# One transformer block on one core: the first V products' squares, 1/rms and second V weights moved, and four small changes of order

## The chip, the cores and the metric

The kernel runs on one core of a Trainium2 chip, as one program. The metric is the device time of one execution in microseconds, as the median of several executions. In the text, PE is TensorE (the matrix engine), ACT is ScalarE, DVE is VectorE, POOL is GpSimd, and SP is SyncE, which issues most of the DMA transfers. P is 128, the number of partitions; SEQ is 512 tokens, in NT = 4 blocks of 128; D is 1024, in KB = 8 blocks of 128.

## The reference, cut to what matters

```
def layer(x, mem):                                   # x (1, 512, 1024), mem (1, 256, 1024), float32
    h = rms_norm(x, g_mix_pre)                       # x * rsqrt(mean(x*x) + eps) * g
    q_f, k_f, v_f, f_logit, q_c, k_c, v_c = split(h @ w_in)   # 512,512,512,8,512,512,512 columns
    log_f = log_sigmoid(f_logit + b_fgate)
    o_f = forgetting_attention(q_f, k_f, v_f, log_f)          # 8 heads of 64, causal
    o_c = chunked_rel_attention(q_c, k_c, v_c, rel_bias)      # 8 heads of 64
    mix = concat(rms_norm(o_f, g_fox_out), rms_norm(o_c, g_chunk_out)) @ w_out
    x = x + rms_norm(mix, g_mix_post)
    h, m = rms_norm(x, g_mem_pre), rms_norm(mem, g_mem_kv)
    ca = cross_attention(h, m, w_mem_q, w_mem_kv, w_mem_o)    # 4 heads of 256, 256 memory tokens
    x = x + rms_norm(ca, g_mem_post)
    h = rms_norm(x, g_ffn_pre)
    g, u = split(h @ w_gate_up)                               # 2 x 2816 columns
    return x + rms_norm((silu(g) * u) @ w_down, g_ffn_post)
```

## The kernel before

**Precision and products.** Every float32 operand of a product is held as two rounded halves, hi and lo (hi is a rounded copy, lo is the difference). `mm3` (line 139) issues three matmuls into one accumulator: hi times hi (L140), and the two mixed ones (L141, L142). For each weight block that arrives by DMA as `raw`, ACT casts the hi half (L125) and DVE subtracts to get the lo half (L126).

**Order.** The program is written as tile code. Tiles come from pools: a tag of a pool has a fixed number of buffers, and a tile that takes a buffer waits until the tile that held it before has been read for the last time. In PSUM there are 8 banks of 512 columns: tag a has three, s and t two each, o one. A scheduler lays the instructions of each engine into one fixed order by its own estimates of when they can run; `later(n)` and the place in the code shift it. At run time each engine goes through its list in order and waits at an instruction until what it reads is there.

**The first stage** (lines 224 to 355) computes the V products of the first head group and the forget gate's logits, before q and k. It needs no 1/rms for that, because 1/rms is a factor of each token that is applied afterwards. It goes through the 8 blocks of 128 features of x: `x_block` makes hTh and hTl (x times the gain, hi on ACT, lo on DVE), `v_weights` splits the 520 weight columns of the block into two halves, 264 and 256 columns wide (`vhi`, `vlo`), and `v_products` issues 24 matmuls per block into six accumulators: four of 264 columns (banks s, s, a, o) and two banks a that hold two of 256 each. Beside it, `squares` squares x on ACT into xs (L287), and the eight squared blocks are summed into one: five sums on POOL (L289), two on DVE (L321, L322). `feature_rstd` then multiplies the sum with a column of ones on PE (L251), adds eps on DVE (L146), raises to the power -1/2 on POOL (L147), and spreads the four columns of 1/rms over all partitions by four matmuls on PE (L258), which ACT copies to rrow (L327). The V accumulators are read out by ACT (L334) and DVE (L335), scaled by 1/rms. Six matmuls on a block of zeros (`still`) come first of all on PE (L237).

The weights of V take both buffers of the tags hi and lo of the pool wp. These are the buffers in which the weights of q and k are split afterwards.

**The attention stage.** `forget_gate` (L432 to 475) computes the log-sigmoid with Abs, Exp and Ln on ACT. A head then adds scores and bias on DVE (L519, which also gives the row's maximum nm), takes Exp on ACT (L529), scales on DVE (L531) and transposes on PE (L534). Exp, Ln and Silu lie in different function tables of ACT, which an ACT_TABLE_LOAD brings in ahead of the first instruction that uses another table.

**The FFN.** Gate and up are computed in column blocks of 256, n = 2 to 21, two for each u = n // 2 from 1 to 10. Those in EIGHT = (2, 3, 11) use eight products (96 matmuls), the others a Strassen-like scheme of seven products (`seven`, 84 matmuls). A `product` is four `mm3`, k = 0 to 3, of 128 x 256 each: its weights lie in a ring (ring_hi, ring_lo), its tokens in b or t1 to t4. ACT and DVE fill the ring ahead of PE (L902, L903), DVE also forms the sums of weights and of products. u = 0 is done apart from weights loaded earlier (first_ffn). The down projection follows; in two places it already cuts one matmul into two along its columns (L1229).

Of the kernel before, what the change touches and what calls it, by code (L numbers as in the profile page):

```python
# [14 lines left out]
P = 128  # L15
# [21 lines left out]
def hybrid_block_kernel(  # L37
# [189 lines left out]
    with tc.tile_pool(name="mix", bufs=1, reuse_waits="tile") as bp:  # L227
# [8 lines left out]
        for j in range(6):  # L236
            pe.matmul(warmed[:, :P], still, still, start=True, stop=True)  # L237
# [9 lines left out]
        def feature_rstd(sq, blocks, n, name):  # L247
# [7 lines left out]
            r = rstd_of(ss[:, :n], n, name)  # L255
# [5 lines left out]
            return r, rb[:, : n * P]  # L261

        vhi = [wp.tile([P, KB, n], F32R, tag="hi", name=f"vhi{n}", bufs=2) for n in (264, 256)]
        vlo = [wp.tile([P, KB, n], F32R, tag="lo", name=f"vlo{n}", bufs=2) for n in (264, 256)]
        halves = (slice(256, 520), slice(0, 256))

        def v_weights(raw, k, n):
            for j, cs in enumerate(halves):
                h = vhi[j][:, k : k + n, :]
# [4 lines left out]
            for j, cs in enumerate(halves):  # L274
                dve.tensor_tensor(
                    out=vlo[j][:, k : k + n, :], in0=raw[:, :, cs], in1=f32(vhi[j][:, k : k + n, :]), op=ALU.subtract
                )
# [8 lines left out]
        def squares(k, n):  # L286
            act.activation(xs[:, k : k + n, :], xt[:, k : k + n, :], AF.Square, scale=1.0 / 32.0)  # L287
            for j in range(max(k, 1), min(k + n, KB - 2)):
                pool.tensor_tensor(out=xs[:, 0, :], in0=xs[:, 0, :], in1=xs[:, j, :], op=ALU.add)  # L289

        def v_products(k):
            for t in range(NT):
                ts = slice(t * P, (t + 1) * P)
                mm3(acc0[t][:, :264], hTh[:, k, ts], hTl[:, k, ts], vhi[0][:, k, :], vlo[0][:, k, :], k == 0, k == KB - 1)
            for t in range(NT):
# [3 lines left out]
                    vhi[1][:, k, :], vlo[1][:, k, :], k == 0 and t % 2 == 0, k == KB - 1 and t % 2 == 1,  # L299
# [10 lines left out]
        for k, n in ((0, 1), (1, 1), (2, 2), (4, 2), (6, 2)):  # L310
# [123 lines left out]
        def forget_gate():  # L434
# [12 lines left out]
            act.activation(u, u, AF.Ln)  # L447
            dve.tensor_tensor(out=e, in0=e, in1=u, op=ALU.add)
# [126 lines left out]
        def mem_norm():  # L575
            mrow = feature_rstd(msq, range(2), 2, "rm")[1]
# [67 lines left out]
    with tc.tile_pool(name="cross", bufs=1, reuse_waits="tile") as cp:  # L644
# [163 lines left out]

        xr = mix
# [579 lines left out]
```

## Time and profile before

| | us |
|---|---|
| runs: lowest, median, highest of 3 | 779.17, 785.84, 786.11 |
| the profiled execution | 786.02 |
| its span, first to last instruction | 784.1 |
| outside the span | 1.9 |

The stages of the profiled execution follow one another as follows: first V products 5.7 to 35 us, q and k and the two attentions to about 245, memory projections, output projection and cross-attention to about 435, gate and up of the FFN 435 to 663, down 663 to 777, and the end to 784. A timeline row gives the start of an instruction from the span's start, its duration, engine, line, operation, output and inputs, shape, and how many neighbours of the same kind were joined; in brackets how long the engine had been idle before it, and what ended that. PE's instructions overlap in their records: the time that one costs in a stream is the distance from its start to the next one's start, called its step below.

### The profile page before, as it was taken

The numbers are of one execution on the slowest core, as the hardware profiler recorded it, in microseconds if no ns is written. First come the engines' busy times: TensorE is split into PE (matmuls) and PEld (weight loads), VectorE is DVE, ScalarE is ACT, GpSimd is POOL, SyncE is SP. The second block draws the span as 40 slices with busy tenths as digits, with TensorE's granted clock in tenths as the row PEclk, the third lists the DMA queues.
The fourth block names the chain that finished last, engine by engine and source line by source line (L and its number), as shares of the span: only waits on it lengthen the run. The fifth ranks groups of instructions, "written<-read, shape, count | busy, mean of one in ns | idle before, by whom it ended". The sixth has DMA issues, their size and how long they took to land.

```text
span 784.1 us, 12865 instructions
## 1 busy us (share of the span) xinstructions
PE 763.6 (97%) x4996; PEld 683.5 (87%) x4996; DVE 597.9 (76%) x1089; ACT 429.7 (55%) x781; POOL 70.9 (9%) x110
## 2 busy tenths in 40 slices
PE   8899999999999999999999999999999999999996
PEld 8887788888778988877778899999999999898985
DVE  5567889879887588645563778998899998987736
ACT  7358888757886348444553635554344446454421
POOL 6001231110321101000001100000000000000001
PEclk9999999999999999999999999999999999999999
DMA  6241212412312734421350202332433332323222
GB/s 245 79 137 54 55 55 67 130 67 82 114 60 96 276 107 163 131 72 64 107 171 18 81 28 81 108 109 81 135 109 108 108 109 77 111 92 124 89 74 107
DMA packets 60748, 80.05 MB, mean 102 GB/s; under 512 B 2704, under 2 KB 43664, under 8 KB 60688
## 3 DMA queue, kind: packets, MB, share of 16 engines
q1 hardware_dynamic: 59264, 74.49, 29.5%
q0 software_dynamic: 1280, 4.72, 1.6%
q8 instruction: 39, 0.64, 0.3%
q14 instruction: 21, 0.17, 0.1%
q10 hardware_dynamic: 144, 0.02, 0.0%
HBM read 77.13 MB, written 2.10 MB: 101 GB/s over the span
## 4 chain that ended last, share of the span: by engine, by line
PE 81%; ACT 6%; DVE 5%; issue 3%; DMA 2%; POOL 2%; SPq 0%; DVEq 0%; POOLq 0%; ACTq 0%
PE ps_a L141 15%; PE ps_a L142 15%; PE ps_a L140 15%; PE ps_s L140 5%; PE ps_s L141 5%; PE ps_s L142 5%; PE ps_t L141 2%; PE ps_t L140 2%; PE ps_t L142 2%; PE ps_o L140 2%; PE ps_o L141 2%; PE ps_o L142 2%; PE ps_t L534 2%; DMA raw<-in_dram 2%; PE ps_o L543 2%
## 5 line engine op out<-in xcount | busy, mean ns | idle before, releaser
L902 ACT CAST ring_hi<-fraw 128x1024 fp32r<-128x1024 f32 (+1 forms) x62 | 57.5, 931 | 65.1 <-DVE fraw L981 16.2
L126 DVE TENSOR_TENSOR lo<-raw,hi 128x1024 fp32r<-128x1024 f32 x56 | 68.2, 1223 | 22.2 <-ACT hi L125 21.8
L903 DVE TENSOR_TENSOR ring_lo<-fraw,ring_hi 128x1024 fp32r<-128x1024 f32 (+1 forms) x62 | 66.4, 1074 | 18.4 <-ACT ring_hi L902 17.9
L142 PE MATMUL ps_a<-hTh,lo 128*128 128x512 f32 x192 | 76.8, 400 | 0.6 <-DVE lo L126 0.6
L140 PE MATMUL ps_a<-hTh,hi 128*128 128x512 f32 x192 | 75.8, 395 | 0.2 <-ACT hi L125 0.2
L141 PE MATMUL ps_a<-hTl,hi 128*128 128x512 f32 x192 | 75.9, 395 | 0.0
L125 ACT CAST hi<-raw 128x1024 fp32r<-128x1024 f32 x56 | 57.8, 1048 | 23.8 <-PE ps_a L141 15.0
L902 ACT CAST ring_hi<-sums 128x1024 fp32r<-128x1024 f32 x34 | 35.7, 1049 | 52.5 <-PE ps_t L141 17.0
L903 DVE TENSOR_TENSOR ring_lo<-sums,ring_hi 128x1024 fp32r<-128x1024 f32 x34 | 41.4, 1218 | 4.0 <-ACT ring_hi L902 4.0
L142 PEld LDWEIGHTS ps_a<-hTh,lo 128*128 128x128 f32 x192 | 36.1, 188 | 7.3 <-DVE lo L126 1.0
L141 PEld LDWEIGHTS ps_a<-hTl,hi 128*128 128x128 f32 x192 | 36.1, 188 | 6.4
L140 PEld LDWEIGHTS ps_a<-hTh,hi 128*128 128x128 f32 x192 | 36.2, 188 | 6.0 <-ACT hi L125 0.4
L529 ACT ACTIVATE p<-p,nm 128x128 f32<-128x128 f32 (+1 forms) x64 | 36.1, 565 | 8.4 <-DVE nm L519 7.6
L140 PE MATMUL ps_a<-b,ring_hi 128*128 128x256 f32 x140 | 39.4, 281 | 0.0
L141 PE MATMUL ps_a<-b,ring_hi 128*128 128x256 f32 x140 | 39.3, 281 | 0.0
L142 PE MATMUL ps_a<-b,ring_lo 128*128 128x256 f32 x140 | 39.3, 281 | 0.0
L140 PE MATMUL ps_s<-b,ring_hi 128*128 128x256 f32 x128 | 36.0, 281 | 0.0
L141 PE MATMUL ps_s<-b,ring_hi 128*128 128x256 f32 x128 | 36.0, 281 | 0.0
L142 PE MATMUL ps_s<-b,ring_lo 128*128 128x256 f32 x128 | 36.0, 281 | 0.0
L536 ACT CAST pth<-ps_t 128x128 fp32r<-128x128 f32 (+1 forms) x64 | 27.1, 425 | 14.5 <-PE ps_t L534 13.7
L537 DVE TENSOR_TENSOR ptl<-ps_t,pth 128x128 fp32r<-128x128 f32 (+1 forms) x64 | 30.7, 486 | 5.1 <-ACT pth L536 3.8
L534 PE MATMUL ps_t<-ident,p 128*128 128x128 f32 x160 | 28.1, 275 | 1.1 <-DVE p L531 0.8
(541 smaller groups left out, 2642.5 us busy)
## 6 DMA issues: line engine op xcount, KB each, us to landing
raw<-in_dram SPq DMA_DIRECT2D x64, 512.0 KB, 3.7
fraw<-in_dram SPq DMA_DIRECT2D x62, 512.0 KB, 3.5
cb<-in_dram SPq DMA_DIRECT2D x8, 256.0 KB, 2.7
xo<-in_dram POOLq DMA_DIRECT2D x4, 512.0 KB, 5.4
out_dram<-yd SPq DMA_DIRECT2D x8, 256.0 KB, 2.0
rawv<-in_dram SPq DMA_DIRECT2D x3, 520.0 KB, 6.9
xt<-in_dram SPq DMA_DIRECT2D x3, 512.0 KB, 7.7
gb<-in_dram POOLq DMA_DIRECT2D x3, 512.0 KB, 4.4
```

What stands on the lines that cost most here:

```text
L125: act.copy(hi[:, j : j + n, :], raw)
L126: dve.tensor_tensor(out=lo[:, j : j + n, :], in0=raw, in1=f32(hi[:, j : j + n, :]), op=ALU.subtract)
L140: pe.matmul(dst, sh, mh, start=first, stop=False)
L141: pe.matmul(dst, sh, ml, start=False, stop=False)
L142: pe.matmul(dst, sl, mh, start=False, stop=last)
L529: act.activation(p[:, :n], p[:, :n], AF.Exp, bias=nm, scale=-1.0, accum_out=sm)
L534: pe.transpose(tp[:, k * P : (k + 1) * P], p[:, k * P : (k + 1) * P], ident)
L536: act.copy(span(ph, i), t3)
L537: dve.tensor_tensor(out=span(pl, i), in0=t3, in1=f32(span(ph, i)), op=ALU.subtract)
L543: pe.matmul(acc[:, a:], v[:, k, vh, :], m[:, k * PTS + a : k * PTS + SEQ], start=k == 0 and m is ph, stop=k == NT - 1 and m is pl,)
L902: act.copy(h2, v)
L903: dve.tensor_tensor(out=l2, in0=v, in1=f32(h2), op=ALU.subtract)
```

## The change

The change has one large part and four small ones.

1. **Squares, 1/rms and V weights.** The squares of x are taken in pairs of blocks (that of blocks 0 and 1 only when block 1 is there), and are added by three DVE additions of 128x1024 instead of five on POOL and two on DVE; two squared blocks are left, so that the product with ones is eight matmuls instead of four. These are issued after the V products of block 6, and the spread of 1/rms after those of block 7. The second half of the V weights (256 columns) goes into two tiles of four blocks each, in buffers of the tags T and Q of the attention's pool, so that one of the two buffers of hi and of lo is free for the first weights of q.
2. Ten matmuls on zeros at the start instead of six.
3. An Exp of one column directly behind the Ln of the forget gate.
4. A Silu of one column ahead of the stage of w_o.
5. In the FFN, for u = 1, 2, 4 and 7, the first L142 matmul of the gate's first product is cut into two matmuls of 128 columns.

```
-        for j in range(6):
+        for j in range(10):
...
-            r = rstd_of(ss[:, :n], n, name)
+            return rstd_of(ss[:, :n], n, name)
+
+        def spread(r, n):
...
-        vhi = [wp.tile([P, KB, n], F32R, tag="hi", name=f"vhi{n}", bufs=2) for n in (264, 256)]
-        vlo = [wp.tile([P, KB, n], F32R, tag="lo", name=f"vlo{n}", bufs=2) for n in (264, 256)]
+            return rb[:, : n * P]
+
+
+        vhi, vlo = (
+            [[wp.tile([P, KB, 264], F32R, tag=tag, name=f"v{tag}264", bufs=2)]]
+            + [[bp.tile([P, 4, 256], F32R, tag=own, name=f"v{tag}256_{j}", bufs=3) for j in range(2)]]
+            for tag, own in (("hi", "T"), ("lo", "Q"))
+        )
...
-        def squares(k, n):
-            act.activation(xs[:, k : k + n, :], xt[:, k : k + n, :], AF.Square, scale=1.0 / 32.0)
-            for j in range(max(k, 1), min(k + n, KB - 2)):
-                pool.tensor_tensor(out=xs[:, 0, :], in0=xs[:, 0, :], in1=xs[:, j, :], op=ALU.add)
+        def squares(k):
+            act.activation(xs[:, k : k + 2, :], xt[:, k : k + 2, :], AF.Square, scale=1.0 / 32.0)
+
+        def add_squares(k, other):
+            a = xs[:, k : k + 2, :]
+            dve.tensor_tensor(out=a, in0=a, in1=xs[:, other : other + 2, :], op=ALU.add)
...
-            if k < 4:
-                squares(k, n)
-            if k == 2:
-                squares(4, 2)
-                squares(6, 2)
-                dve.tensor_tensor(out=xs[:, KB - 2, :], in0=xs[:, KB - 2, :], in1=xs[:, KB - 1, :], op=ALU.add)
-                dve.tensor_tensor(out=xs[:, 0, :], in0=xs[:, 0, :], in1=xs[:, KB - 2, :], op=ALU.add)
+            if k:
+                squares(k if k > 1 else 0)
+            if k in (2, 6):
+                add_squares(k - 2, k)
+            if k == 6:
+                add_squares(0, 4)
             for j in range(k, k + n):
                 v_products(j)
-            if k == 4:
-                rcol, rps = feature_rstd(xs, (0,), NT, "rx")
-                act.copy(rrow, rps)
+                if j == 6:
+                    rcol = feature_rstd(xs, range(2), NT, "rx")
+        act.copy(rrow, spread(rcol, NT))
...
             act.activation(u, u, AF.Ln)
+            act.activation(warm, u[:, :1], AF.Exp)
...
+        act.activation(mix_ms[:, 0, 0:1], sm[:, :1], AF.Silu)
         xr = mix
...
+                pe.matmul(dst, w[0][:, k, :], b[:, 0, k, :], start=first and k == 0, stop=False)
+                pe.matmul(dst, w[0][:, k, :], b[:, 1, k, :], start=False, stop=False)
+                for to in parts:
+                    pe.matmul(dst[:, to], w[1][:, k, :], b[:, 0, k, to], start=False, stop=last and k == 3)
...
+            whole, parts = (slice(0, 256),), IN_STEP if u in (1, 2, 4, 7) else (slice(0, 256),)
```

DVE's list in the first stage, from the lo half of x of blocks 2 and 3 on. Before (L281 is that lo half, L275 the lo half of the V weights, L321 and L322 the additions of squares):

```order
L281 SCALAR_TENSOR_TENSOR hTl<-xt,gn,hTh 128x512 x2
L275 TENSOR_TENSOR vlo_110<-rawv_119,vhi_108 128x528
L275 TENSOR_TENSOR vlo_111<-rawv_119,vhi_109 128x512
L281 SCALAR_TENSOR_TENSOR hTl<-xt,gn,hTh 128x512
L321 TENSOR_TENSOR xs<-xs 128x512
L281 SCALAR_TENSOR_TENSOR hTl<-xt,gn,hTh 128x512
L322 TENSOR_TENSOR xs<-xs 128x512
L275 TENSOR_TENSOR vlo_110<-rawv_251,vhi_108 128x528
L275 TENSOR_TENSOR vlo_111<-rawv_251,vhi_109 128x512
```

The same stretch of DVE now (L291 and L285 are the lo halves, L301 the additions, L126 the lo half of the first q weights):

```order
L291 SCALAR_TENSOR_TENSOR hTl<-xt,gn,hTh 128x512 x2
L301 TENSOR_TENSOR xs<-xs 128x1024
L285 TENSOR_TENSOR vlo_115<-rawv_125,vhi_112 128x528
L285 TENSOR_TENSOR vlo_0_116<-rawv_125,vhi_0_113 128x512
...
L285 TENSOR_TENSOR vlo_115<-rawv_248,vhi_112 128x528
L285 TENSOR_TENSOR vlo_1_117<-rawv_248,vhi_1_114 128x512
L301 TENSOR_TENSOR xs<-xs 128x1024
L285 TENSOR_TENSOR vlo_115<-rawv_307,vhi_112 128x528
L285 TENSOR_TENSOR vlo_1_117<-rawv_307,vhi_1_114 128x512
L301 TENSOR_TENSOR xs<-xs 128x1024
L126 TENSOR_TENSOR lo_427<-raw_0_428,hi_426 128x1024
L126 TENSOR_TENSOR lo_427<-raw_4_432,hi_426 128x1024
```

No addition stands directly ahead of the third pair of weight halves (blocks 4 and 5) any more, one stands ahead of the second pair (blocks 2 and 3), and the lo halves of q's first weights have come forward to the end of the V weights.

PE's list around the product of the squares with ones, before (ps_s, ps_a and ps_o are V accumulators, L251 the product with ones, L258 the spread):

```order
L142 MATMUL ps_a_100<-vhi_109,hTl 128x256
L251 MATMUL ps_t_309<-ones,xs 128x1 x4
L140 MATMUL ps_s_95<-vhi_108,hTh 128x264
L141 MATMUL ps_s_95<-vlo_110,hTh 128x264
L142 MATMUL ps_s_95<-vhi_108,hTl 128x264
L140 MATMUL ps_s_96<-vhi_108,hTh 128x264
L258 MATMUL ps_t_317<-ident,rx_314 128x128 x4
L141 MATMUL ps_s_96<-vlo_110,hTh 128x264
```

The same rows of PE now, with the 24 V products of block 7 in between, and the first q product (hi_426, lo_427) behind them:

```order
L142 MATMUL ps_a_100<-vhi_1_114,hTl 128x256
L251 MATMUL ps_t_344<-ones,xs 128x1 x8
L140 MATMUL ps_s_95<-vhi_112,hTh 128x264
...
L142 MATMUL ps_a_100<-vhi_1_114,hTl 128x256
L260 MATMUL ps_t_380<-ident,rx_353 128x128 x4
L140 MATMUL ps_a_446<-hTh,hi_426 128x512
L141 MATMUL ps_a_446<-hTl,hi_426 128x512
L142 MATMUL ps_a_446<-hTh,lo_427 128x512
```

Four matmuls stood between the product with ones and the spread; now a whole block of 24 does, and the spread is the last thing ahead of q.

ACT's list where the first head begins, before (fb is the bias of a head, p its scores):

```order
L459 CAST c_605<-fc 8x512
L485 ACTIVATE fb_0_626<-ps_s_624,ct 128x128
L485 ACTIVATE fb_1_631<-ps_s_624,ct 128x256
L485 ACTIVATE fb_2_636<-ps_s_624,ct 128x384
L485 ACTIVATE fb_3_641<-ps_s_624,ct 128x512
L529 ACT_TABLE_LOAD
L529 ACTIVATE p_0_649,sm_651<-p_0_649,nm_650 128x128
```

And ACT's list at the forget gate now, some twenty rows earlier (fe and fu are its small tiles, L458 the Ln, L459 the new Exp):

```order
L451 ACTIVATE fe_588<-z 128x32
L452 ACTIVATE fe_588<-fe_588 128x32
L458 ACT_TABLE_LOAD
L458 ACTIVATE fu_589<-fu_589 128x32
L459 ACT_TABLE_LOAD
L459 ACTIVATE warm_93<-fu_589 128x1
L417 ACTIVATE Q_473<-qk 64x512 x2
```

The table load has left the head's first Exp and stands behind the Ln, ahead of the scaling of Q.

PE's list at the start of u = 2 in the FFN now (the gate's first product; before, the third row was one matmul of 128x256):

```order
L1084 MATMUL ps_a_5080<-b_4278,ring_hi 128x256
L1085 MATMUL ps_a_5080<-b_4278,ring_hi 128x256
L1087 MATMUL ps_a_5080<-b_4278,ring_lo 128x128 x2
L1084 MATMUL ps_a_5080<-b_4278,ring_hi 128x256
L1085 MATMUL ps_a_5080<-b_4278,ring_hi 128x256
```

Nothing else moves there: the neighbours and their sizes are those of before, and one matmul has become two.

## Rows read from the trace of the kernel before

**Rows 1.** The page, busy time of each engine (share of the span, instructions).

```profile
PE 763.6 (97%) x4996; PEld 683.5 (87%) x4996; DVE 597.9 (76%) x1089; ACT 429.7 (55%) x781; POOL 70.9 (9%) x110
```

**Rows 2.** Waits of PE, whole span: total, times, longest, in us.

```profile
PE ps_s L515 <- DVE nm L519: 1.7, 3, 1.2
```

**Rows 3.** First stage: length, busy of PE, PEld, DVE, ACT, POOL; granted clock, DMA.

```profile
1.05:3.98 2.93, 2.93 (x12) 2.63 (x12) 0.00 (x0) 1.65 (x3) 0.32 (x2) 1.00 0.63 212
3.98:5.67 1.69, 0.00 (x0) 0.03 (x1) 1.10 (x4) 1.08 (x2) 0.00 (x0) 1.00 1.00 316
5.67:9.29 3.62, 3.62 (x16) 3.62 (x17) 3.24 (x7) 3.02 (x6) 1.94 (x5) 1.00 0.98 358
9.29:18.92 9.63, 9.63 (x82) 9.63 (x81) 6.29 (x8) 8.63 (x14) 8.94 (x11) 1.00 0.69 243
```

**Rows 4.** Timeline of PE at the third pair of V weights.

```profile
18.93 0.28 PE L140 MATMUL ps_s<-vhi,hTh 128*128 128x264 f32 x1
20.27 0.39 PE L141 MATMUL ps_s<-vlo,hTh 128*128 128x264 f32 x1 [1.06 <-DVE vlo L275]
```

**Rows 5.** Timeline of DVE over the additions of squares and V weights.

```profile
10.97 2.06 DVE L275 TENSOR_TENSOR vlo<-rawv,vhi 128x528 fp32r<-128x528 f32 x2 [0.41 <-ACT vhi L273]
...
18.91 0.69 DVE L322 TENSOR_TENSOR xs<-xs 128x512 f32<-128x512 f32 x1 [2.90 <-POOL xs L289]
...
22.06 1.30 DVE L275 TENSOR_TENSOR vlo<-rawv,vhi 128x528 fp32r<-128x528 f32 x2
```

**Rows 6.** Timeline of PE from the product with ones to the spread.

```profile
26.06 0.95 PE L251 MATMUL ps_t<-ones,xs 128*128 128x1 f32 x8
...
27.32 0.28 PE L140 MATMUL ps_s<-vhi,hTh 128*128 128x264 f32 x1
28.39 1.16 PE L258 MATMUL ps_t<-ident,rx 128*128 128x128 f32 x8 [0.78 <-POOL rx L147]
```

**Rows 7.** Timeline of PE from the last V product into q.

```profile
34.56 0.28 PE L142 MATMUL ps_a<-vhi,hTl 128*128 128x256 f32 x1
...
36.32 0.50 PE L142 MATMUL ps_a<-hTh,lo 128*128 128x512 f32 x1 [0.59 <-DVE lo L126]
```

**Rows 8.** Timeline of all engines at the first Exp of the heads.

```profile
66.58 1.28 ACT L529 ACT_TABLE_LOAD   x1
...
67.88 0.40 ACT L529 ACTIVATE p<-p,nm 128x128 f32<-128x128 f32 x1
...
68.40 0.16 DVE L530 RECIPROCAL rc<-sm 128x1 f32<-128x1 f32 x1 [2.27 <-ACT p L529]
...
69.01 0.50 PE L515 MATMUL ps_s<-T,Q 128*128 128x512 f32 x1 [1.22 <-DVE nm L519]
```

**Rows 9.** Timeline of ACT at the first Silu.

```profile
457.12 1.28 ACT L1095 ACT_TABLE_LOAD   x1 [3.95 <-PE ps_a L142]
```

**Rows 10.** Busy time by stretches of gate and up, and of down (columns as in rows 3).

```profile
484.08:663.34 179.26, 179.26 (x1524) 179.26 (x1523) 164.40 (x238) 87.74 (x132) 0.00 (x0) 1.00 0.32 102
686.05:709.05 23.00, 23.00 (x205) 23.00 (x204) 18.87 (x31) 12.52 (x18) 0.00 (x0) 1.00 0.34 115
```

**Rows 11.** Timeline of PE at the first cut in down.

```profile
685.36 0.33 PE L1229 MATMUL ps_s<-ring_hi,latex 128*128 128x128 f32 x2
685.53 0.33 PE L140 MATMUL ps_s<-ring_hi,latex 128*128 128x256 f32 x1
685.71 0.28 PE L141 MATMUL ps_s<-ring_lo,latex 128*128 128x256 f32 x1
```

**Rows 12.** Timeline of PE at the last weights' arrival ahead of u = 1.

```profile
455.45 0.41 PE L141 MATMUL ps_a<-b,gate_w 128*128 128x256 f32 x2
455.70 0.28 PE L142 MATMUL ps_a<-b,gate_w 128*128 128x256 f32 x1
```

**Rows 13.** Busy time by stretches of 20 us, gate and up, then down.

```profile
600.00:620.00 20.00, 20.00 (x173) 20.00 (x171) 19.03 (x28) 9.42 (x14) 0.00 (x0) 1.00 0.34 107
680.00:700.00 20.00, 20.00 (x156) 19.11 (x155) 19.47 (x36) 11.28 (x16) 0.00 (x0) 1.00 0.21 72
```

More of the change, by code (lines that the diff above doesn't have):

```diff
@@ L268, in v_weights @@
             for j, cs in enumerate(halves):
-                h = vhi[j][:, k : k + n, :]
+                h = at_block(vhi[j], k, n)
                 if k == 0:
@@ L275, in v_weights @@
                 dve.tensor_tensor(
-                    out=vlo[j][:, k : k + n, :], in0=raw[:, :, cs], in1=f32(vhi[j][:, k : k + n, :]), op=ALU.subtract
+                    out=at_block(vlo[j], k, n), in0=raw[:, :, cs], in1=f32(at_block(vhi[j], k, n)), op=ALU.subtract
                 )
@@ L298, in v_products @@
                     acc1[t // 2][:, (t % 2) * 256 : (t % 2 + 1) * 256], hTh[:, k, ts], hTl[:, k, ts],
-                    vhi[1][:, k, :], vlo[1][:, k, :], k == 0 and t % 2 == 0, k == KB - 1 and t % 2 == 1,
+                    at_block(vhi[1], k)[:, 0, :], at_block(vlo[1], k)[:, 0, :], k == 0 and t % 2 == 0, k == KB - 1 and t % 2 == 1,
                 )
@@ L575, in mem_norm @@
         def mem_norm():
-            mrow = feature_rstd(msq, range(2), 2, "rm")[1]
+            mrow = spread(feature_rstd(msq, range(2), 2, "rm"), 2)
             for k in range(KB):
@@ L1065, in hybrid_block_kernel, with product @@
                         )
-        def product(dst, w, b, first=True, last=True):
+        def product(dst, w, b, first=True, last=True, parts=(slice(0, 256),)):
             for k in range(4):
-                mm3(dst, w[0][:, k, :], w[1][:, k, :], b[:, 0, k, :], b[:, 1, k, :], first and k == 0, last and k == 3)
+                if k:
+                    parts = (slice(0, 256),)
+                pe.matmul(dst, w[0][:, k, :], b[:, 0, k, :], start=first and k == 0, stop=False)
+                pe.matmul(dst, w[0][:, k, :], b[:, 1, k, :], start=False, stop=False)
+                for to in parts:
+                    pe.matmul(dst[:, to], w[1][:, k, :], b[:, 0, k, to], start=False, stop=last and k == 3)
+        IN_STEP = (slice(0, P), slice(P, 256))
         left, right = slice(0, 256), slice(256, 512)
@@ L1081, in up_eight, with eight @@
             return done
-        def eight(tags, done):
+        def eight(tags, done, parts):
             accs = [bank(tag) for tag in tags]
@@ L1089, in eight @@
                     for n, ns in enumerate((left, right)):
-                        product(accs[m][:, ns], w, bs[n], half == 0 and n == 0, half == 1 and n == 1)
+                        begin = half == 0 and n == 0
+                        product(accs[m][:, ns], w, bs[n], begin, half == 1 and n == 1, *([parts] if begin and m == 0 else []))
                     if half:
@@ L1118, in twice, with seven @@
             return bass.AP(a.tensor, a.offset, [list(a.ap[0]), [0, 2], list(a.ap[-1])])
-        def seven(O, tags, done):
+        def seven(O, tags, done, parts):
             p17, p26, p35, p4 = (bank(tag) for tag in tags)
@@ L1124, in seven @@
             (a11,) = take()
-            product(p17[:, left], a11, b11)
+            product(p17[:, left], a11, b11, parts=parts)
             act.copy(v, p17[:, left])
@@ L1160, in hybrid_block_kernel @@
         for u in range(1, FB // 2):
+            whole, parts = (slice(0, 256),), IN_STEP if u in (1, 2, 4, 7) else (slice(0, 256),)
             if 2 * u in EIGHT:
-                eight(("a", "a"), gate_eight)
+                eight(("a", "a"), gate_eight, parts)
             else:
-                seven(G, ("a", "a", "a", "o"), gate_seven)
+                seven(G, ("a", "a", "a", "o"), gate_seven, parts)
             dst = hidden(u)
             if 2 * u + 1 in EIGHT:
-                eight(("s", "s"), up_eight(dst))
+                eight(("s", "s"), up_eight(dst), whole)
             else:
-                seven(U, ("s", "s", "t", "t"), up_seven(dst))
+                seven(U, ("s", "s", "t", "t"), up_seven(dst), whole)
             keep(u, dst)
```

6 lines of the change are left out of this document (4 added, 2 removed).

## The prediction

> **What bounds the kernel now.** I read the page's busy times first: PE is busy for 97% of the span, DVE for 76%, ACT for 55% [rows 1]. So the end is set by PE, and only three things can move it: a wait of PE that goes, a matmul that becomes cheaper or superfluous, and a step (start to next start) that gets shorter at the same shape. The view of PE's waits comes next; its longest entry is 1.7 us in three times, one of 1.2 us [rows 2]. No wait is large, so the change is worth what its small waits add up to, and each has to be read from a timeline. Waits hide one thing: PE that works slowly counts as busy. So I also divided the length of long stretches by their matmuls, and found two speeds twice, at the start [rows 3] and in the FFN [rows 10].
>
> **V products: what goes.** Four losses stand in the first stage.
>
> Clock. The first 16 matmuls took 3.62 us, 0.226 each, the 82 records behind them 9.63, about 0.12 each with the records at the edges taken off [rows 3]. Columns of 256 and 264 in 0.22 us are the lower of PE's two clock levels (1.2 GHz), in 0.11 to 0.12 the upper (2.4 GHz), though the granted clock is printed as 1.00 in all four rows. Ahead of the 16, PE had worked for 2.93 us on zeros (twelve records) and then stood for 1.69. With four more matmuls on zeros, at 2.93/6 = 0.49 each, that gap shrinks by 1.95, so to nothing. I expect the upper level from about the first real matmul: 16 x (0.226 - 0.120) = 1.7, of which 0.3 is the start of the stream itself, leaves 1.4. Bounds: 0, if the clock rises no earlier, and 1.7.
>
> Third pair of weights. One step of 1.34 us instead of 0.12, and 0.1 for the slow restart [rows 4]: 1.3. The chain behind it is on DVE: the weights' lo half stood behind the addition L322, which had waited 2.90 us for POOL [rows 5]. That addition is now elsewhere and POOL is out of it.
>
> 1/rms. The spread waited for POOL's power: 28.39 - 27.32 = 1.07 instead of 0.12 [rows 6], 0.95. Now 24 matmuls, 2.9 us, stand between the product with ones and the spread, against the 2.3 us that the same way took here (26.06 to 28.39). I take 1.0 with the restart.
>
> Start of q. From the last V product to the third q matmul 1.76 us passed [rows 7], for one V step (0.12) and two of 512 columns (twice 0.23, double the 256-column steps of rows 10): 1.18 lost, because q's weights could only be split when V's buffers were free. They are now split before V ends. Something of a new product's start stays: 1.1.
>
> **V products: what comes.** The product with ones has twice the matmuls: 0.95 more [rows 6], take 0.9. The DVE additions cost PE nothing where a weight half isn't late for it: three of 128x1024, which I put at 1.2 each by the subtraction of 1,040 columns in 1.30 (22.06, rows 5). The tight place is block 2. By hand, with the clock up, PE ends block 1 near 11.6 and first takes six hi matmuls of block 2, to 12.35; its lo half is done near 12.3, since an addition stands ahead of it but the half itself takes 0.65 without POOL's additions, where it took 1.03 beside them (half of 2.06, against half of 1.30, rows 5). Cost 0, up to 1 if the addition is late. The squares are complete near 20.7 and PE asks at 26.2. The sum is 1.4 + 1.3 + 1.0 + 1.1 - 0.9 = **3.9 us** (2.0 to 4.8).
>
> **Exp table.** The load takes 1.28 us ahead of the first head's Exp; DVE and then PE wait for that chain, PE for 1.22 us [rows 8]. Moved behind the Ln, it stands ahead of the scaling of Q, which the heads read only after it, on an ACT that is busy for 55% of the span [rows 1]. Gain **1.25** (0, if another wait takes its place, to 1.4).
> The Trainium skill ("ScalarE: Activation LUTs", section "What ACT_TABLE_LOAD costs") states a drain of about 1.38 us beside the 1.28 of the load itself. Here the next ACTIVATE starts 1.30 us behind the load's start (67.88 after 66.58, rows 8), so no drain shows and I count the load alone; by the page the sum would be 1.4 us better.
>
> **Silu table.** At its old place ACT had been idle for 3.95 us and PE isn't made to wait [rows 9], so moving it saves nothing. At the new one it stands in the end of the cross-attention, where it delays a copy that w_o's products follow; other w_o products are put ahead of these. Cost between 0 and the load's own 1.28: take **-0.2**, since PE's list has cover there.
>
> **The cuts in the FFN.** The same 128x256 matmul has two steps. From 484.08 to 663.34 PE took 1,522 matmuls (1,524 records less two that overlap the edges) in 179.26 us: 117.8 ns. From 686.05 to 709.05 it took 203 in 23.00: 113.3 ns [rows 10]. Neither stretch has a wait. What happened just ahead of the second: a matmul was cut into two of 128 columns (685.36), and soon behind it the steps are 0.11 [rows 11]. What put PE into the longer step is two matmuls in 0.25 at 455.45, a short delay; from there on it is 0.12 [rows 12]. I read this as two rhythms of weight load and matmul, of which an odd step in the stream picks one, and which then holds until the next disturbance. The cut is placed at u = 1, 2, 4, 7. If it puts PE into the short rhythm for u = 2 to 10, the gain is 1,522 x 4.5 ns = 6.85. Each cut costs: 685.36 to 685.71 is 0.35 for two matmuls' work against 0.236, so 0.11, four times 0.45. u = 1 (241 matmuls, 1.1 us) I leave out: its cut may stand ahead of the disturbance at 455.45.
> DVE takes something back. It was busy for 19.03 of 20 us from 600 to 620 [rows 13]; PE 3.8% faster wants the same in 19.24. That just fits, but u = 2 and 3 and the passage into down (19.47 of 20, rows 13) don't leave room: 0.5, between 0 and 2. Sum 6.85 - 0.45 - 0.5 = **5.9** (3.5 to 7.5).
>
> **The total.** 3.9 + 1.25 - 0.2 + 5.9 = 10.85 from the profiled execution's 786.02: **775.2 us**. That execution lies 0.2 above the median of the runs (785.84), so nothing is corrected. One of the three runs gave 779.17, 6.7 below the median, which is just what the short rhythm would save in gate and up; I read it as the kernel falling into that rhythm by chance, and as a sign that it can be held.
>
> **Rivals.**
> *The cuts don't choose the rhythm.* For it: one cut followed by short steps is one case, and rhythms may be set by where operands lie or by a later DVE wait. Then the FFN gives -0.45 instead of 5.9 and the time is 775.2 + 6.35 = 781.5. Chance 0.17.
> The Trainium skill ("TensorE: Matmul & The Clock Gate", section "Back-to-back issue gap") gives a single gap of N/2.4 + 2.5 ns: 109 ns for 256 columns and 112 for two of 128, so a cut could only cost, which is this rival's result. The trace shows two steps for one shape (113.3 and 117.8, rows 10) where that rule has one, so I give it less weight than the row.
> *A cut turns the rhythm rather than setting it.* Then u = 2 and 3 run short, u = 4 to 6 long, u = 7 to 10 short: (336 + 672) x 4.5 ns = 4.5 less 0.45: 1.8 less gain, 777.0. Against it speaks that nothing in the trace shows a cut that ends the short rhythm. 0.08.
> *DVE becomes the bound.* With PE in the short rhythm from 484 on, weights for down come too late around 660 to 701, where DVE has only half a microsecond in 20 left [rows 13]. A wait also throws PE back into the long rhythm until the next cut. I price it at 2.5 us more than counted: 777.7. 0.10.
> *Slower: the squares hold PE.* The eight matmuls with ones now stand in PE's list ahead of all of block 7, and wait for the third DVE addition, which is behind the weights of blocks 6 and 7 and their Square on ACT. From 26.2 us on, each us by which that addition ends later is lost in full. It eats the change's whole gain when it ends at 37, and I see it end near 20.7, so this needs DVE or a DMA to be 16 us later than before: time 787 or more. 0.03.
> That the clock doesn't rise earlier gives 776.6 and lies within the forecast.
>
> **How the numbers follow.** The forecast itself has 0.62. What can be told from no change is 1%, 7.86 us: faster below 778.0, slower above 793.7. Faster collects the forecast (0.62), the turning rhythm (0.08) and about half of the DVE rival (0.05): 0.75. Same is 0.22, slower 0.03. The low end takes the good ends of all terms, 4.8 + 1.4 + 0 + 7.5 = 13.7, so 772.3, rounded to 772.0; the high end must hold the first rival: 781.6. What is left out is the slower rival, above, and the first rival together with a bad V stage.
>
> **What would show it.** In the changed kernel's profile: the first V matmuls step 0.12 and not 0.22; no wait of PE for the lo half near 18 us or for 1/rms; q's first matmul near 31.8 instead of 35; PE's wait for nm behind the first Exp gone; no new wait near 393; the stretch from u = 2 to u = 10 at 113 ns per matmul, some 172.5 us long; no waits of PE for ring_lo there or at 690. The prediction is wrong if that stretch still shows 118, or if its rows show PE idle behind DVE.

## The result, and the profile after

The changed kernel took 776.87 us (median of 8 runs, 776.01 to 778.97), the kernel before 786.07 beside it (8 runs, 779.17 to 789.06): a ratio of 0.9886, 95% interval 0.9870 to 0.9902, so faster by 1.1%. The forecast was 775.2, with a range of 772.0 to 781.6. The profiled execution took 778.66, at the slow end of its eight, with a span of 776.9 instead of 784.1.

The page's busy times of the changed kernel: PE works 3.7 us less, and its share has risen from the 97% of [rows 1] to 98%.

```profile
PE 759.9 (98%) x5016; PEld 680.2 (88%) x5016; DVE 598.1 (77%) x1090; ACT 429.2 (55%) x782; POOL 63.8 (8%) x105
```

**First stage.** PE's timeline of the changed kernel, with the first V product, the product with ones, the spread, and the first q product. These answer to [rows 4, 6, 7].

```profile
6.47 0.78 PE L140 MATMUL ps_s<-vhi,hTh 128*128 128x264 f32 x2 [0.78 <-DVE vhi L281]
...
28.64 1.84 PE L251 MATMUL ps_t<-ones,xs 128*128 128x1 f32 x16
...
33.30 1.05 PE L260 MATMUL ps_t<-ident,rx 128*128 128x128 f32 x8
34.16 0.47 PE L140 MATMUL ps_a<-hTh,hi 128*128 128x512 f32 x1
```

From 6.47 to 34.16 no row has a wait in brackets: the waits for the third pair of weights, for 1/rms and for q's weights are gone. But the first product starts 0.8 later than the 5.67 of [rows 3], and the clock has not come earlier. The stretch of [rows 3] in the changed kernel (length, busy of PE, PEld, DVE, ACT and POOL, then the granted clock, the DMA share and GB/s):

```profile
5.67:9.29 3.62, 2.84 (x14) 2.85 (x14) 3.62 (x9) 3.62 (x7) 0.69 (x3) 1.00 1.02 379
```

14 matmuls began in the 2.82 us after 6.47, about 0.2 each, which is the lower clock level (1.2 GHz), although the row prints a granted clock of 1.00, as [rows 3] did. Why the product starts late is seen on DVE (the first row is the kernel before, the second the changed kernel) and on POOL of the changed kernel:

```profile
5.24 0.49 DVE L271 CAST vhi<-rawv 128x264 fp32r<-128x264 f32 x2
```

```profile
4.99 1.52 DVE L281 CAST vhi<-rawv 128x264 fp32r<-128x264 f32 x2
```

```profile
4.72 0.52 POOL L395 MEMSET L<- 64x512 f32 x1
5.18 0.52 POOL L466 MEMSET fzero<- 8x512 f32 x1
5.65 0.52 POOL L470 MEMSET c<- 128x512 f32 x1
```

Two casts of 128x264 take 1.52 us while POOL fills tiles with zeros; in the kernel before POOL stood waiting for the squares then, until 7.29, and they took 0.49. This side of taking the additions off POOL I had not priced.

**Exp table.** ACT's timeline at the first head: the Exp follows the bias directly, with no load between them, as there was in [rows 8]. The bias began at 64.78 in the kernel before (first row below), so the first stage has given 1.7 us up to here.

```profile
64.78 1.78 ACT L485 ACTIVATE fb<-ps_s,ct 128x128 f32<-128x128 f32 x4 [1.96 <-PE ps_s L480]
```

```profile
63.09 1.78 ACT L497 ACTIVATE fb<-ps_s,ct 128x128 f32<-128x128 f32 x4 [2.00 <-PE ps_s L492]
64.75 0.42 ACT L541 ACTIVATE p<-p,nm 128x128 f32<-128x128 f32 x1
```

**Silu table.** ACT's timeline, then PE's, at the end of the cross-attention. The load pushes the last cast of the probabilities back, and PE's step from 392.99 to 393.47 is 0.48 instead of 0.23: 0.25 us lost.

```profile
390.50 1.28 ACT L821 ACT_TABLE_LOAD   x1
...
392.84 0.58 ACT L806 CAST pt<-ps_t 128x512 fp32r<-128x512 f32 x1
```

```profile
392.99 0.40 PE L140 MATMUL ps_a<-woh,oT 128*128 128x512 f32 x1
393.47 0.50 PE L140 MATMUL ps_o<-pt,vm 128*128 128x512 f32 x1
```

**Gate and up.** Busy times by stretches, u = 1 and then u = 2 to 10, as in [rows 10]:

```profile
452.94:481.68 28.74, 28.74 (x247) 28.74 (x245) 22.34 (x25) 11.00 (x14) 0.00 (x0) 1.00 0.22 65
481.68:654.80 173.12, 173.12 (x1527) 172.97 (x1526) 162.33 (x235) 86.65 (x131) 0.00 (x0) 1.00 0.34 106
```

u = 1 ran at 117 ns per matmul, the rest at 113.5 (173.12 over 1,525 records, three of them second halves of cut matmuls): 6.1 us less than the 179.26 of before. The cut at u = 4 in PE's timeline stands inside a stream that is already short and stays short:

```profile
519.78 0.28 PE L1085 MATMUL ps_a<-b,ring_hi 128*128 128x256 f32 x1
519.89 0.33 PE L1087 MATMUL ps_a<-b,ring_lo 128*128 128x128 f32 x2
520.06 0.33 PE L1084 MATMUL ps_a<-b,ring_hi 128*128 128x256 f32 x1
...
520.47 0.28 PE L1084 MATMUL ps_a<-b,ring_hi 128*128 128x256 f32 x1
```

From 519.89 to 520.47 four matmuls' work takes 0.58 instead of 0.45, so the cut costs 0.13; the next 512 steps are 0.113 again. So a cut doesn't turn the rhythm. The profiles of all kernels with cuts agree: behind u = 1's first product, a cut found PE in the long step (117.4 to 117.8) eight times and in the short one 24 times, and each time the stretch behind it stepped 113.3 to 113.5.

**Down.** There 1.3 us are given back: the end of gate and up came 8.5 us earlier (654.80 after 663.34), the end of the span 7.2. PE's timeline shows the largest wait, and a window the DVE that is behind it:

```profile
693.39 0.28 PE L140 MATMUL ps_s<-ring_hi,latelo 128*128 128x256 f32 x1
694.32 0.39 PE L141 MATMUL ps_s<-ring_lo,latelo 128*128 128x256 f32 x1 [0.65 <-DVE ring_lo L916]
```

```profile
660.00:672.00 12.00, 12.00 (x54) 9.94 (x54) 12.00 (x22) 7.01 (x9) 0.57 (x1) 1.00 0.39 133
```

### The profile page after: what moved, and what is told of

It reads as the page before. It is cut to its first block, busy times and chain, and to the rows that moved or that the text cites. A ratio compares the mean times of both kernels' runs of the same rounds, so it can differ in the third digit from the quotient of the medians.

```text
span 776.9 us, 12898 instructions
## 1 busy us (share of the span) xinstructions
PE 759.9 (98%) x5016; PEld 680.2 (88%) x5016; DVE 598.1 (77%) x1090; ACT 429.2 (55%) x782; POOL 63.8 (8%) x105
## 4 chain that ended last, share of the span: by engine, by line
PE 72%; DVE 13%; ACT 7%; issue 4%; DMA 4%; POOL 0%; DVEq 0%; POOLq 0%; ACTq 0%
PE ps_a L141 12%; PE ps_a L142 12%; PE ps_a L140 12%; DVE ring_lo L916 3%; PE ps_a L1087 2%; PE ps_a L1084 2%; PE ps_a L1085 2%; PE ps_s L140 2%; PE ps_s L141 2%; PE ps_s L1084 2%; PE ps_s L1085 2%; PE ps_s L1087 2%; PE ps_s L142 2%; PE ps_t L546 2%; DMA fraw<-in_dram 2%
## 5 line engine op out<-in xcount | busy, mean ns | idle before, releaser
L126 DVE TENSOR_TENSOR lo<-raw,hi 128x1024 fp32r<-128x1024 f32 x56 | 68.2, 1224 | 22.0 <-ACT hi L125 21.7
L142 PE MATMUL ps_a<-hTh,lo 128*128 128x512 f32 x192 | 76.6, 399 | 0.0
L142 PEld LDWEIGHTS ps_a<-hTh,lo 128*128 128x128 f32 x192 | 36.1, 188 | 6.3
L1087 PE MATMUL ps_a<-b,ring_lo 128*128 128x256 f32 (+1 forms) x144 | 39.2, 276 | 0.0
```

Source lines behind the costliest of these rows:

```text
L126: dve.tensor_tensor(out=lo[:, j : j + n, :], in0=raw, in1=f32(hi[:, j : j + n, :]), op=ALU.subtract)
L142: pe.matmul(dst, sl, mh, start=False, stop=last)
L1087: pe.matmul(dst[:, to], w[1][:, k, :], b[:, 0, k, to], start=False, stop=last and k == 3)
```

## The experiments

Twelve kernels ran in three batches, each batch on one chip with runs of the kernel before beside it. That kernel fell into two groups there: of its 87 runs in all, 45 took 777.3 to 781.5 (median 779.5) and 42 took 785.2 or more (median 786.2), with 17 of 23 in the longer group in the first batch, 14 of 34 in the second and 4 of 22 in the third. So I compare medians in us, and say of the kernel before which group is meant.

**The four cuts alone, and the V stage alone.** Both start from the kernel before; the first takes only `product`, `seven` and `eight` from the change, the second only the first stage's part, with six matmuls on zeros.

> The kernel before with the four cuts of the FFN alone. Theory: a cut puts PE into the short step and it stays there, so gate and up from u = 2 take 173 us instead of 179.3 (6.2 gained), and down gives 1 to 1.5 of it back in waits for ring_lo that DVE fills: 786.1 becomes 781.1 to 781.6. Rival (the V stage's shift, not the cuts, changed the rhythm): the stretch stays at 117.8 ns per matmul and the time at 786.

Measured: 780.35 (12 runs, 779.01 to 782.91), where the kernel before had 6 runs near 779.75 and 17 near 786.2. That is below the 781.1 to 781.6 of the theory, and no run fell into the longer group. Busy times of its profile from the cut of u = 2 up to 617, and of a short stretch behind 636; then PE's timeline at 641:

```profile
484.95:617.20 132.25, 132.24 (x1166) 132.04 (x1165) 122.72 (x176) 64.33 (x97) 0.00 (x0) 1.00 0.34 105
636.29:640.40 4.11, 4.11 (x37) 4.11 (x36) 2.88 (x5) 2.55 (x3) 0.00 (x0) 1.00 0.02 6
```

```profile
641.27 0.39 PE L1074 MATMUL ps_a<-thi,ring_lo 128*128 128x256 f32 x1 [0.58 <-DVE ring_lo L903]
```

The first stretch steps 113.6 ns (1,164 matmuls), so the rival is out: the cuts alone choose the rhythm. Behind 617 DVE makes PE wait inside gate and up as well, 0.58 us at 641. Behind a late matmul at 636 PE steps 117 ns for some 35 matmuls (second row), and behind the wait at 641 it is at 113.5 again, with no cut near. So a late step or a wait can move the rhythm too, either way. Against the kernel before's shorter group the cuts gain nothing; by medians they cost it some 0.6.

> The kernel before with the V stage's part alone (squares, 1/rms, V weights), six matmuls on zeros as before, no Exp, Silu or cuts. Theory from the trace after: the part gives 1.7 us, since the clock's part of my sum (1.4) does not come and the first product starts 0.8 later: 784.4. Rival: without the ten matmuls on zeros it gives the predicted sum without the clock, 2.5: 783.6. No gain at all would be 786.1.

Measured: 783.73 (12 runs), but as two groups: 5 runs near 779.2 and 7 near 784.0. Against the longer group of the kernel before the part gave 2.2 us (784.0 lies between my 784.4 and the rival's 783.6), against the shorter, with 5 and 6 runs, some 0.5; why less there is not shown. In the profile, an execution of 783.91, the whole of u = 1 to 10 is in the long rhythm:

```profile
453.70:661.00 207.30, 207.30 (x1763) 207.30 (x1762) 186.36 (x262) 100.03 (x146) 0.00 (x0) 1.00 0.32 97
```

That is 117.7 ns per matmul (1,761): an execution of the longer group is in the long rhythm, as that of [rows 10] was. The V part doesn't remove it; the groups are still there without the cuts, 4.8 us apart. No execution of a shorter group without cuts was profiled, so that it is the short rhythm there rests on the size of the gap and on its vanishing with a cut.

**POOL's memsets held back.** Ahead of each of the memsets of the L tiles, of fzero and of c stands a one-column POOL operation on the cast that was slowed:

```
+        def held(a):
+            v = f32(vhi[1][0][: a.shape[0], 0, 0:1])
+            pool.tensor_tensor(out=a, in0=v, in1=v, op=ALU.mult)
...
+            held(l[:, 0, 0:1])
             pool.memset(f32(l[H1, 0, :]), 0.0)
```

> The changed kernel, with POOL's memsets of the first stage held until DVE has cast the first block's V weights (five one-column POOL operations that read that cast stand ahead of them). Theory: the memsets, no longer queued behind the additions of squares, run at 4.1 to 6.1 us beside DVE's casts and slow them (1.52 us for two instead of 0.49); held back, the first V product starts near 5.6 instead of 6.47 and the time falls by 0.8, from 776.9 to 776.1; if the clock then rises earlier too, by up to 1.4 more, 774.7. Rival: the casts were late because the first V weights landed late; then the first product stays near 6.4 and the time at 776.9.

Measured: 776.16 (6 runs). Its timelines of DVE and of PE, and its window after 5.67:

```profile
5.22 0.49 DVE L281 CAST vhi<-rawv 128x264 fp32r<-128x264 f32 x2
```

```profile
5.66 0.56 PE L140 MATMUL ps_s<-vhi,hTh 128*128 128x264 f32 x1
```

```profile
5.67:9.29 3.62, 3.62 (x26) 3.62 (x26) 2.99 (x8) 3.56 (x7) 3.22 (x8) 1.00 1.02 381
```

The casts take 0.49 again and PE starts at 5.66: the theory holds for the casts and the start. In all ten other profiles of the new V stage with the memsets early, the first product starts at 6.45 to 6.47; in this one and in the last one below, at 5.66 and 5.54. Little of the 0.8 lasts: the first six products step 0.22 here, up to 7.05, and q begins at 32.11, only 0.2 before the 32.34 of the changed kernel's second profile (below), in which the clock was up at the first product. The median fell by 0.7 against the first 776.87 and by 0.3 against the 776.46 of the third batch.

**Without the early Silu.** The one line is taken out.

> The changed kernel without the one-column Silu ahead of the stage of w_o. Theory: the table load there delays the last cast of the probabilities by 0.85 us, of which PE waits 0.25: 776.6, with the load back ahead of the first gate's Silu, where PE does not wait. Rival: the load's new place pays for itself elsewhere (the first gate's Silu sooner): 776.9 or more.

Measured: 775.83 (6 runs, 774.72 to 778.6), 1.0 below the changed kernel's. But its profile shows another thing too: u = 1 ran short by itself.

```profile
450.65:478.19 27.54, 27.54 (x245) 27.54 (x244) 22.21 (x25) 12.28 (x15) 0.00 (x0) 1.00 0.20 60
```

243 matmuls in 27.54 us are 113.3 ns. That is worth 1.1 and comes and goes from execution to execution, so the Silu's own price is the 0.25 of the trace; the median doesn't prove it.

**Without the early Exp.** The line behind the Ln is taken out.

> The changed kernel without the one-column Exp behind the Ln. Theory: the table load is back ahead of the first head's Exp, where PE waits 1.2 us for it: 776.9 + 1.4 = 778.3, with the wait of PE for nm at 68 us back at 1.2. Rival: another wait takes its place in the changed kernel, and the time stays at 776.9.

Measured: 777.77 (12 runs). PE's waits in its profile have the entry of [rows 2] back, with the same 1.2, where the changed kernel's longest for nm is 0.3:

```profile
PE ps_s L526 <- DVE nm L530: 1.7, 3, 1.2
```

So the term stands. By medians it is 0.9 to 1.3 (against 776.87 and 776.46).

**One cut instead of four**, at u = 2.

> The changed kernel with the cut at u = 2 alone. Theory: one cut puts PE into the short step and no later work of gate and up takes it out, so the stretch from u = 2 to u = 10 stays at 113.3 ns and the time falls by the three cuts saved, 0.3: 776.6. Rival (the rhythm falls back and each cut renews it): some of the stretch is at 117.8 and the time up to 4.5 us longer, 781.

Measured: 776.49 (11 runs, 774.38 to 778.43). The whole of u = 2 to 10 in its profile:

```profile
480.09:652.00 171.91, 171.91 (x1519) 171.91 (x1518) 161.81 (x236) 86.25 (x132) 0.00 (x0) 1.00 0.34 106
```

113.3 ns over 1,517 matmuls: a single cut held PE in the short rhythm for 172 us, and the other three are not needed in such an execution.

**Six matmuls on zeros instead of ten.**

> The changed kernel with six matmuls on zeros at the start, as before, instead of ten. Theory: in the profiles so far the clock rose at 9.3, 10.5, 6.4, 6.9 and 5.0 us, with six or ten, so the count does not set it; the median stays within 0.7 of 776.9. Rival (ten bring the upper level earlier by the gap they close): 1.4 longer, 778.3.

Measured: 778.1 (12 runs, 775.5 to 780.44), 1.6 above the cut_once runs on the same chip, of which some 0.4 are the three cuts that those runs save. My expectation said no difference; the rival's 1.4 was nearer. The profile shows how: its granted clock is 0.78 in the window after 5.67. PE begins its products fast and falls back at 7.78, after the standstill of 2.47 us that the six zeros had left ahead of 6.46:

```profile
5.67:9.29 3.62, 2.83 (x17) 2.86 (x18) 3.62 (x9) 3.62 (x7) 0.68 (x3) 0.78 1.01 380
```

```profile
7.51 0.28 PE L142 MATMUL ps_s<-vhi,hTl 128*128 128x264 f32 x1
7.63 0.35 PE L141 MATMUL ps_a<-vlo,hTh 128*128 128x264 f32 x1
7.78 0.42 PE L142 MATMUL ps_a<-vhi,hTl 128*128 128x264 f32 x1
```

From there its steps are 0.22 up to 11.0, and q begins at 33.83, 1.5 later than in the changed kernel's second profile. v_only, also with six, shows the same 0.78. Of the ten profiles with ten zeros, six have the first V products at about 0.12 from the start, two have steps of 0.22 until about 7, and two, the changed kernel's first profile among them, until about 10.

**The late sums on POOL.** In late_seven the four additions go from DVE to POOL:

```
-            dve.tensor_tensor(out=f[:, 3], in0=f[:, 1], in1=f[:, 3], op=ALU.add)
+            pool.tensor_tensor(out=f[:, 3], in0=f[:, 1], in1=f[:, 3], op=ALU.add)
...
```

> The changed kernel with the sums of late_seven (20 additions of 128x256 between 655 and 690 us) on POOL instead of DVE. Theory: DVE is the bound there, it is busy 12.0 and 11.7 of 12 us, and PE waits some 1.1 us for ring_lo; with 6.8 us taken off DVE these waits go: 775.8. Rival: POOL's additions slow DVE's while both run, as the additions of squares did in the kernel before, or are late themselves: 777 or more.

Measured: 788.01 (12 runs, 787.0 to 791.4), 11 us slower than the changed kernel. Timelines of POOL, ACT and PE:

```profile
655.11 1.60 POOL L1218 TENSOR_TENSOR gf<-gf 128x256 f32<-128x256 f32 x1
```

```profile
656.75 1.04 ACT L1210 CAST latex<-gf 128x1024 fp32r<-128x1024 f32 x1 [2.89 <-POOL gf L1218]
657.70 1.99 ACT L915 CAST ring_hi<-fraw 128x1024 fp32r<-128x1024 f32 x2
...
687.14 1.04 ACT L1210 CAST latev<-f 128x1024 fp32r<-128x1024 f32 x1 [5.16 <-POOL f L1218]
688.09 1.04 ACT L915 CAST ring_hi<-fraw 128x1024 fp32r<-128x1024 f32 x1
```

```profile
658.79 0.49 PE L140 MATMUL ps_a<-ring_hi,g 128*128 128x512 f32 x1 [1.91 <-ACT ring_hi L915]
...
689.19 0.58 PE L140 MATMUL ps_s<-ring_hi,latex 128*128 128x256 f32 x1 [4.21 <-ACT ring_hi L915]
```

One sum takes 1.60 us here on POOL, against 0.42 on DVE. ACT waits 2.89 us for it, and the cast of the next ring weights, which PE needs, stands behind that on ACT: PE waits 1.91 us at 658.79. At 687 the same order costs PE 4.21 us. Both halves of my rival came true: the sums are late themselves, and DVE's subtractions of 128x1024 at 653 and 655 took 1.49 and 1.43 us beside them instead of 1.22. So the run doesn't tell whether a DVE with less to do would end the waits of down: it put a new wait in their place.

**The changed kernel beside the last three.**

> The changed kernel as it is, beside the three below on one chip, since the kernel before fell into two groups of times that differ by 6.8 us and its share in each differs by chip. Theory: the changed kernel stays in one group, 775.5 to 779, median 776.9; the ratio to the kernel before depends on how many of that kernel's runs are in the long rhythm. Rival: the changed kernel too shows runs near 783.

Measured: 776.46 (11 runs, 775.53 to 779.46); the kernel before beside it had 18 of 22 runs near 779.5, so the ratio was 0.9956 there (0.9934 to 0.9979). The 19 runs of the changed kernel in its two batches lie in one group, as do all runs of the kernels with a cut (late_pool's aside, which has its own place): none of 100 is above 783. This second profile is one in which the clock was up at the first product:

```profile
26.81 1.84 PE L251 MATMUL ps_t<-ones,xs 128*128 128x1 f32 x16
...
32.34 0.47 PE L140 MATMUL ps_a<-hTh,hi 128*128 128x512 f32 x1
```

q begins at 32.34, 1.8 before the first profile's 34.16, with the same start of PE at 6.47.

**The cut of u = 1 later.** It moves to the second product, behind the wait at 453; u = 4 and 7 lose theirs.

```
-                        product(accs[m][:, ns], w, bs[n], begin, half == 1 and n == 1, *([parts] if begin and m == 0 else []))
+                        product(accs[m][:, ns], w, bs[n], begin, half == 1 and n == 1, *([parts] if half == 0 and n == 1 and m == 0 else []))
...
-            whole, parts = (slice(0, 256),), IN_STEP if u in (1, 2, 4, 7) else (slice(0, 256),)
+            whole, parts = (slice(0, 256),), IN_STEP if u in (1, 2) else (slice(0, 256),)
```

> The changed kernel with the cut of u = 1 moved to its second product, which stands behind the wait that puts PE into the long step at 453 us, and without the cuts at u = 4 and 7. Theory: u = 1 (240 matmuls) then runs at 113.3 instead of 117.8 in every execution, 1.1 less, and two cuts fewer save 0.2: 775.6. Rival: as two profiles show, u = 1 is short by chance already in part of the runs, so the median falls by half of that, to 776.2; or the wait comes later than the cut, then no change.

Measured: 775.78 (5 runs). Stretches of its profile ahead of the cut and behind it, and the cut in PE's timeline:

```profile
449.39:460.50 11.11, 11.11 (x96) 11.11 (x96) 7.83 (x13) 2.30 (x4) 0.00 (x0) 1.00 0.15 47
461.04:480.90 19.86, 19.86 (x178) 19.86 (x177) 17.69 (x18) 9.31 (x11) 0.00 (x0) 1.00 0.19 56
```

```profile
460.22 0.33 PE L1087 MATMUL ps_a<-b,ring_lo 128*128 128x128 f32 x2
```

118 ns (94 matmuls) before, 113 (176) behind. In this execution the cut came at 460.22 and moved PE from the long step into the short one, in a stretch that was long in the changed kernel's profiles; the part of u = 1 ahead of it stayed long. The median fell by 0.7, between the theory and its rival.

**Four matmuls with ones instead of eight.**

```
                 add_squares(0, 4)
+                dve.tensor_tensor(out=xs[:, 0, :], in0=xs[:, 0, :], in1=xs[:, 1, :], op=ALU.add)
...
-                    rcol = feature_rstd(xs, range(2), NT, "rx")
+                    rcol = feature_rstd(xs, (0,), NT, "rx")
```

> The changed kernel with one more DVE addition (128x512) that leaves a single block of squares, so that the product with ones is four matmuls instead of eight. Theory: PE is behind nothing there and the squares are complete 8 us early, so PE saves the half of 1.7 us: 776.9 - 0.85 = 776.0. Rival: the q weights' lo half behind that addition is late, and the gain is lost: 776.9.

Measured: 776.81 (12 runs), no gain. The product with ones did take half as long, and the spread began 0.89 earlier than in after_beside (30.59 after 31.48). In this profile PE then fell out of the short rhythm at 612, behind one late step (0.17 at 611.80) and with no cut after it:

```profile
612.09:653.50 41.41, 41.41 (x354) 41.41 (x353) 39.45 (x61) 22.14 (x36) 0.00 (x0) 1.00 0.32 103
```

41.41 us over 352 matmuls are 117.6 ns, 1.5 us lost, and the waits for ring_lo in down don't appear, which saves 1.2. The profile as a whole is 1.0 shorter than that of after_beside: 0.9 shorter up to q, 1.1 longer from there to down, 1.2 shorter behind. The median shows no gain; why it doesn't is open.

**What helped, together.** Held memsets, no early Silu, cuts at u = 1 (late) and u = 2, four matmuls with ones.

> The changed kernel with what helped put together: POOL's memsets held (0.7), no early Silu (0.25), the late cut of u = 1 with one more at u = 2 (1.3), four matmuls with ones (0.85). If the parts add: 776.9 - 3.1 = 773.8. Rival: the earlier V stage and the short rhythm in u = 1 only bring forward the wait for ring_lo in down, which takes back 1 to 2: 775.3.

Measured: 774.93 (5 runs, 774.11 to 775.16), 1.5 below the changed kernel beside it and 0.9941 (0.9929 to 0.9953) of the kernel before, which was mostly in its shorter group there. It is the fastest median of all, and half of the sum of its parts: the rival's 775.3 is nearer than 773.8. Its profile, the shortest of its five runs, has u = 1 to 10 at 113 ns throughout, u = 1 already ahead of the late cut, and still a wait for DVE's ring_lo in down:

```profile
688.68 0.28 PE L140 MATMUL ps_s<-ring_hi,latelo 128*128 128x256 f32 x1
689.24 0.38 PE L141 MATMUL ps_s<-ring_lo,latelo 128*128 128x256 f32 x1 [0.29 <-DVE ring_lo L923]
```

That wait is shorter than the changed kernel's 0.65, so the rival's reason doesn't account for the missing half. From the first matmul of down to the end of the span, four profiles took 120.8 to 120.9 us (the kernel before, v_only, six_zeros, four_ones) and nine 121.7 to 122.1, whether down began at 650.4 (together, 121.7) or at 658.9 (cuts_only, 122.1); late_pool is left out. So down gives back 0.9 to 1.4 us or nothing, and not more to a PE that comes earlier.

## Why the prediction was right

**The rhythm (5.9 forecast).** Right, and shown: cuts_only alone empties the longer group, cut_once holds the short step over 1,517 matmuls, and the long step is there without cuts (v_only). In the profile the gain was 6.1 up to the end of gate and up. The reading of the run at 779.17 as the same rhythm by chance is borne out by the two groups, 6.7 us apart, which remain in v_only (4.8 apart there) and vanish with any cut. What I missed is how common the chance is: half of the runs of the kernel before are in the shorter group. So this term is a gain only against the other half: the changed kernel's 776.5 (19 runs) is 9.7 below the longer group and 3.0 below the shorter one.

**What DVE gives back (0.5 forecast, 0 to 2).** Too small: 1.3 in the profile, almost all in down, at the place that the rival named (DVE busy 12.0 of 12 us from 660); in cuts_only gate and up has such waits too. It is not there in every execution: six_zeros, with u = 1 to 10 all at 113 ns, shows no wait in down. So it explains neither four_ones, which had none either, nor the missing half of together's sum, which stays open; the same kernel's two profiles differ by 1.1 us between q and down, more than most of these parts. That DVE is the cause is read from what PE's waits name and not tested: the one run that took work off DVE made a slower wait.

**V products (3.9 forecast).** Three of four losses went as said: no wait for the third weights, for 1/rms or for q remains. The term that failed in the first profile is the clock (1.4 forecast, none there). The gap that ten matmuls were to close stayed open, at 0.78 us there and 1.48 in after_beside, where the upper level came all the same. It is a matter of the single execution: with ten zeros, six of ten profiles have the upper level at the first product, as forecast, and six_zeros cost 1.2 to 1.6, so the term holds in the median. What I hadn't counted is the 0.8 by which POOL's memsets, through DVE's first casts, delay the first product. The first profile's 1.7 is, to 0.1: 1.3 + 1.0 + 1.1 - 0.9 - 0.8 = 1.7, and no gain by the clock. With q 1.8 earlier in after_beside, it is 3.5 there.

**Exp (1.25) and Silu (-0.2).** The load's move gave 1.4 at the first head in the profile (the offset grew from 1.7 to 3.1) and brought the wait back when undone. The Trainium skill ("ScalarE: Activation LUTs", section "What ACT_TABLE_LOAD costs") states a drain of about 1.38 us beside the load; by an estimate from that the gain would have been 1.4 us more. The trace does not show that: behind the load at 390.50 the next ACTIVATE begins 1.30 us after the load's start, as in [rows 8]. Silu cost 0.25.

**The sum.** 10.85 was forecast from 786.02; medians give 9.2 between 786.07 and 776.87. Had the runs shown been mostly of the shorter group, as in the third batch, the same terms would have come to 3.3 us, inside 1%, and the forecast's sign of "faster by over 1%" would have been wrong with every mechanism right. That the runs of the result were seven of eight in the longer group was luck.

**The rivals.** That the cuts don't choose the rhythm, and that they turn it, are both refuted. The Trainium skill ("TensorE: Matmul & The Clock Gate", section "Back-to-back issue gap") gives the formula that I took for the first rival as the gap of an isolated matmul; by it a cut can only cost. Here, in a stream, one shape has two steps, 113.3 and 117.8 ns, and a cut chose between them. DVE as the bound is half right: the waits came, but those of the first profile, at 637, 688 and 694, did not throw PE back into the long rhythm, while that of cut_once at 691 did, for the 64 matmuls of that shape behind it (117.8). The squares never held PE: the last addition ended at 20.1 in the profile, PE asked at 28.6.

## What to carry to other kernels

When a long stretch of PE shows no waits, divide its length by its matmuls: a few nanoseconds per matmul can be two rhythms of the same stream, and then the runs fall into two groups, so look at every run and not at the median, and ask which group a comparison is with. Taking work from an engine lets its next instructions run earlier, and they can get in the way of another engine that has just become critical: place what follows too. Where two executions of one kernel differ by a microsecond by themselves, a median of a few runs doesn't price a change of some tenths: follow it in the trace, stage by stage, and see how much of it is left at the next stage's start, as 0.2 of the 0.8 of the memsets was.

## What the runs showed of the hardware

A stream of 128x256 products steps 113.3 or 117.8 ns for hundreds of matmuls, and one matmul cut into two of 128 columns moved it from the longer to the shorter (u1_late_cut: 118 before, 113 behind), while a cut in the short one leaves it there. A late step or a wait can move it too: into the longer at 612 in four_ones, into the shorter behind the wait at 641 in cuts_only, and the waits of the first profile left it as it was. What in the engine makes the two rhythms is not shown.

DVE's plain cast of 128x264 beside POOL's memsets took three times as long (1.52 for two instead of 0.49), while the three-operand instruction that makes hTl took 0.75 beside them, as in the kernel before without them; DVE's subtractions beside POOL's additions were also slower before (half of 2.06 against half of 1.30, [rows 5]; 1.49 and 1.43 against 1.22 in late_pool). Memsets themselves stayed at 0.52.

The clock level at the start, by the steps, differs between executions of one kernel: the upper level was there at the first product in after_beside and only about 4 us after it in the first profile, with the same ten matmuls on zeros ahead. After a standstill of 2.5 us behind six of them it was up, and fell back for some 3 us (0.78 granted).
